# Where the split weights of the plain products begin within a 128-byte row

## The chip, the cores and the metric

The kernel runs on one core of a Trainium2 chip, as one launch. The metric is the device time of a launch in microseconds. Times of single instructions come from one profiled execution.

## The reference

One decoder layer for 512 prompt tokens and 64 new tokens (8 sequences of 8), D = 1024, all in float32. Cut to the matrix products:

```python
h = modulate(rms_norm(x, n1_g), sh1, sc1)
x = x + 0.5 * g1 * (silu(h @ w1_gate) * (h @ w1_up)) @ w1_down      # FF = 2816
h = modulate(rms_norm(x, nm_g), sh2, sc2)
u, v, q, k, rv, rg, ga, gb = split(h @ w_in)                        # 10240 columns
o_a = gelu(u) * chunk_spatial_mix(layer_norm(gelu(v)), gm_ws, gm_bs)
o_b = head_rms(retention(rotary(q), rotary(k), rv, S0)) * silu(rg)
x = x + g2 * ((sigmoid(ga) * (o_a @ w_a) + sigmoid(gb) * (o_b @ w_b)) @ w_o)
h = modulate(rms_norm(x, n2_g), sh3, sc3)
x = x + 0.5 * g3 * (silu(h @ w2_gate) * (h @ w2_up)) @ w2_down
y = rms_norm(x, final_g)
```

## The kernel before

All 576 tokens are kept side by side along the free dimension, channels on the partitions. A float32 product is made of three products in the format float32r: each operand is split into a high part (a cast, on ScalarE) and a low part (the rest, on VectorE), and high x high, high x low and low x high are summed in PSUM. Three kinds of split products make up most of the kernel.

The **plain products** are the function `proj` (its matmuls are L482 in the profile). The weights are the stationary operand, 128 x 128 of them for one matmul; the tokens are the moving operand, in two parts of 320 and 256 columns (`PART`). Here belong both down projections, `w_a`, `w_b`, `w_o` and the u columns of `w_in`. Their split weights are made by `load_w` and `split_w` (writes at L184 and L185) or by `Down` (writes at L949 and L954), which takes its tile from `home_wd`, `home_whl`, `home1`, `home_o` or `nine_w`.

The **pairs** are `prod` (L648): gate and up weights, and the columns of `w_in` for q, k and the gates, in a scheme that needs fewer block products. The weights are stationary, 288 token columns move. Their split weights are made by `Weights.put_hi` and `put_lo` (writes at L666 and L676).

The **values** are L1350, L1363 and L1580: tokens stationary, 256 weight columns moving. Their weights come from `load_w`.

Nearly all split weights lie in a tile somewhat larger than they are, and begin `INTO` = 28 elements into it, 112 bytes; `set_in` cuts that piece out. SBUF tiles are laid out so that each of these tiles starts on a multiple of 128 bytes, the pool `line` at the top of the kernel being there for that. Two smaller products of the same format are of use below: L1504 sums squares over the partitions with a tile of ones (`onesr`) as the stationary operand, and L1515 makes the new state of the 64 new tokens.

The built program has these first bytes, modulo 128:

| line | product | columns | stationary begins at | moving begins at |
|---|---|---|---|---|
| L482 | plain | 320 and 256 | 112 | 0 |
| L648 | pairs | 288 | 112 | 0 |
| L1350, L1363, L1580 | values | 256 | 0 | 112 |
| L1504 | squares | 288 | 64 | 0 |
| L1515 | new state | 256 | 0 | 0 |

The order on each engine is set by the program's text and, in three stretches, by an order written out by hand (`BEGIN`, `INTO_MIX`, `INTO_FFN2`). TensorE takes its products in that order, each with a weight load of its own ahead of it, and a product waits for the semaphores of its operands alone. Weights come in through SyncE's queue into the buffers `wraw`.

Of the kernel before, what the change touches and what calls it, by code (L numbers as in the profile page):

```python
# [9 lines left out]
F32R = mybir.dt.float32r  # L10
# [5 lines left out]
P = 128  # L16
D = 1024
KC = D // P
# [8 lines left out]
HEADS = 8  # L27
# [8 lines left out]
GROUPS = (5, 6, 5, 6)  # L36

INTO = 28
HALF = (slice(0, H), slice(H, T))
PART = (slice(0, 320), slice(320, T))  # L40
PW = (320, T - 320)
# [42 lines left out]
def layer_kernel(ctx: ExitStack, tc: tile.TileContext, a):  # L84
# [7 lines left out]
    wp = ctx.enter_context(tc.tile_pool(name="wp", bufs=1))  # L92
# [16 lines left out]
    def nm(s):  # L109
        count[0] += 1  # L110
        return f"{s}_{count[0]}"


    now = {"wraw": None, "slu": None}
    turn = [0, 0]

    def pool(stack, name, side="left"):
        return stack.enter_context(tc.tile_pool(name=nm(name), bufs=1, side=side, reuse_waits="tile"))
# [16 lines left out]

    def nine_w(shape):

        return set_in(now["xs1"], shape, 9 * 256 - shape[1] * shape[2] * shape[3], tag="x", name=nm("xw"), bufs=3)

    def half(dt=F32, w=H):  # L140
        return tp.tile([P, w], dt, tag="h", name=nm("h"), bufs=7)
# [1 line left out]
    def bank():  # L143
        return pp.tile([P, 512], F32, tag="ps", name=nm("ps"), bufs=8)

    def set_in(home, shape, room=INTO, **kw):

        n = 1
        for d in shape[1:]:
            n *= d  # L150
        t = home.tile([P, n + room], F32R, **kw)[:, INTO:INTO + n]
        if len(shape) == 4:
            return t.rearrange("p (a b c) -> p a b c", b=shape[2], c=shape[3])
        return t.rearrange("p (a b c d) -> p a b c d", b=shape[2], c=shape[3], d=shape[4])


    def raw4(shape):
        turn[0] += 1
        own = now["wraw"] is not None and turn[0] % 4 == 0
        return (now["wraw"] if own else wp).tile(  # L160
            [P] + shape, F32, tag="wraw", name=nm("wraw"), bufs=1 if own else 3
        )

    def whl(shape):
        small = len(shape) == 3 and shape[1] == 1
        tag = "whs" if small else "whl"
        return set_in(
            now["whs"] if small else wp, [P] + shape, INTO if small else 64, tag=tag, name=nm(tag), bufs=1 if small else 4
        )

    def load_raw(src, k0, kc, c0, cols):
        raw = raw4([kc, cols])
        nc.sync.dma_start(
            out=raw, in_=src[k0 * P:(k0 + kc) * P, c0:c0 + cols].rearrange("(k p) c -> p k c", p=P)
        )
        return raw

    def high_low(shape):
        t = whl([2] + shape)
        return t[:, 0], t[:, 1]  # L180

    def split_w(raw, eng=None):
        hi, lo = high_low(list(raw.shape[1:]))
        ACT.copy(out=hi, in_=raw)  # L184
        now["lo"] = (eng or DVE).tensor_tensor(out=lo, in0=raw, in1=hi.bitcast(F32), op=ALU.subtract)  # L185
        return hi, lo

    def load_w(src, k0, kc, c0, cols, eng=None):
        return split_w(load_raw(src, k0, kc, c0, cols), eng)

    def split(hi, lo, src):
        ACT.copy(out=hi, in_=src)  # L192
# [36 lines left out]
    def tick(us):  # L229
        for s in list(side):  # L230
            s[1] -= us
            while s in side and s[1] <= 0:
                try:
                    s[1] += next(s[0])
                except StopIteration:
                    side.remove(s)

    def finish(*gens):
        for s in list(side):
            if not gens or s[0] in gens:  # L240
                for _ in s[0]:
                    pass
                side.remove(s)
# [43 lines left out]
    for i in range(2):  # L287
        for n in range(NT):
            rows = P if n < 4 else NS
            t = first.tile([rows, 512], F32, name=nm("xt"))  # L290
            src = a["x_prompt"][0, n * P:(n + 1) * P] if n < 4 else a["x_sample"].rearrange("b l d -> (b l) d")
# [121 lines left out]
    class Norm:  # L413
# [4 lines left out]
        def square(self, x, h):  # L418
            if self.all is None:
                self.all = tp.tile([P, T], F32, tag="all", name=nm("all"), bufs=1)  # L420
                self.acc = [self.all[:, HALF[i]] for i in range(2)]
            first = self.n[h] == 0 and not self.t[h]
            t = self.acc[h] if first else half()
            self.t[h].append(t)
            ACT.activation(out=t, in_=x[:, HALF[h]], func=AF.Square)

# [49 lines left out]
    def proj(w, X, h, kc=KC, c0=0, ks=None, ps=None):  # L476
        ps = bank() if ps is None else ps
        wh, wl = w
        for k in ks or range(kc):
            xh, xl = X[k]  # L480
            for z, (s, m) in enumerate(((wh, xh), (wh, xl), (wl, xh))):
                PE.matmul(  # L482
                    ps[:, :PW[h]], lhsT=s[:, k, c0:c0 + P], rhs=m[:, PART[h]],
                    start=k == 0 and z == 0, stop=k == kc - 1 and z == 2,
                )
        return ps
# [5 lines left out]
    def cost(kc):  # L492
        return kc * 3 * 0.1225
# [26 lines left out]
    class Operands:  # L520
# [27 lines left out]
        def blocks(self, j):  # L548
            hb = self.hb
            return tuple(hb[:, c:c + 2, cl] for c in (2 * j, 4 + 2 * j) for cl in HALF)  # L550

# [56 lines left out]
    def norm_steps(st, n, O, h):  # L608
# [4 lines left out]
        for p in range(4):  # L613
            st[f"x{p}{h}"] = lambda p=p: O.x(p, n.r[h], HALF[h])
            for c in range(2):
                if h:
                    st[f"b{p}{c}"] = lambda p=p, c=c: O.b(2 * p + c, slice(H, NP))
                else:
                    st[f"b{p}{c}0"] = lambda p=p, c=c: O.b(2 * p + c, HALF[0])

# [76 lines left out]
    class Plain(Weights):  # L697
# [43 lines left out]
        def e0s(self):  # L741
            self.g = self.g or self.gated()
            ACT.activation(out=self.g[:, HALF[0]], in_=self.A[0][:, :H], func=AF.Silu)

# [215 lines left out]
            return self.w[c]  # L960

    def home_wd(c, shape):
        return set_in(now["hl"], shape, 64, tag="wd", name=nm("wd"), bufs=2)

    def home_whl(c, shape):
        return home_wd(c, shape) if c in (0, 1, 4, 5) else whl(shape[1:])

    def ffn(xs, wg, wu, wd, gate, p, home, last_down):

# [2 lines left out]
        for i in range(2, FC + 1):  # L972
# [8 lines left out]
            if i in ends:  # L981
                gi = ends.index(i)
                f0, n = i - GROUPS[gi], GROUPS[gi]
                W = Down(wd, f0, n, home if i == FC else home_wd)
                W[0]
                W[1]
            if i > 2:
# [7 lines left out]
            if i == FC:  # L995

                held = {}
                for c, h in LAST[:3]:
                    held[c, h] = proj(W[c], G, h, kc=n, ks=range(n - 1))

                def product(c, h):
                    if (c, h) in held:
                        return proj(W[c], G, h, kc=n, ks=[n - 1], ps=held[c, h])
                    return proj(W[c], G, h, kc=n)

# [118 lines left out]
    win = a["w_in"][0]  # L1124
    U0, V0, Q0, K0, RV0, RG0, GA0, GB0 = 0, 1024, 2048, 3072, 4096, 6144, 8192, 9216
# [5 lines left out]
    def home1(c, shape):  # L1131
        if c in (6, 7):
            return nine_w(shape)
        return home_wd(c, shape) if c in (0, 1, 4, 5) else whl(shape[1:])

    def stream_slots():

# [397 lines left out]

    def weights_b(hds, j):
        kc = 2 * len(hds)
        return load_w(a["w_b"][0], 2 * hds[0], kc, j * (8 // kc) * P, 8 // kc * P)

    def out_b(hds, j, wb, cs=None):  # L1540

# [108 lines left out]
        store()  # L1650

    def weights_u(g):
        return load_w(win, 0, KC, U0 + g * P, P)

    def gate_u(g, wu):
        t = slot([P, T])
# [118 lines left out]
            mix(g - 2)  # L1775
            tick(1.5)
    finish(prev)
    first_a = load_w(a["w_a"][0], 0, KC, 0, P)
    mix(6)
    mix(7)  # L1780
    st.close()
# [9 lines left out]
                nc.sync.dma_start(out=t[c], in_=src[:, c])  # L1791

    def last_b(j):
        wb = load_w(a["w_b"][0], 2 * HEADS - 2, 2, j * 512, 512)
        for c in range(4 * j, 4 * j + 4):
            for h in range(2):
                ps = proj(wb, OBs[HEADS - 1], h, kc=2, c0=c % 4 * P)
                t = acc[c][:, PART[h]]
                DVE.tensor_tensor(out=t, in0=ps[:, :PW[h]], in1=t, op=ALU.add)
            POOL.tensor_tensor(out=acc[c], in0=acc[c], in1=sb[c], op=ALU.mult)  # L1800
# [7 lines left out]

    def home_o(c, shape):
        if c < 2:  # L1810
            return whl(shape[1:])
        if c < 5:
            return nine_w(shape)
        return home_wd(c, shape) if c < 7 else set_in(hb_pool, shape, tag="wo", name=nm("wo"), bufs=1)

    Wo = Down(a["w_o"][0], 0, KC, home_o)
    late = []
# [1 line left out]
    def merge(c, h):  # L1819

        t = sa[c][:, PART[h]]
        DVE.tensor_tensor(out=t, in0=t, in1=acc[c][:, PART[h]], op=ALU.add)
        split(X[c][0][:, PART[h]], X[c][1][:, PART[h]], t)

    for pr in ([0], [1], [2], [3], [4], [5], [6, 7]):
        W = {c: load_w(a["w_a"][0], 0, KC, c * P, P) if c else first_a for c in pr}
        if len(pr) == 2:
            Wo[0]
            Wo[1]
        for h in range(2):  # L1830
            for c in pr:
                ps = proj(W[c], OA, h)
                t = sa[c][:, PART[h]]
                DVE.tensor_tensor(out=t, in0=ps[:, :PW[h]], in1=t, op=ALU.mult)
                if len(pr) == 2:
                    merge(c, h)
                tick(cost(KC))
        if len(pr) == 1:
            late.append(pr[0])
        if pr[0] in (1, 3):  # L1840
            last_b(pr[0] // 2)
        if pr[0] == 2:
            fetch_gates(range(4, KC))
        if pr[0] > 1:
            for c in late[:1 if pr[0] < 5 else KC]:
                late.remove(c)
                for h in range(2):
                    merge(c, h)
# [18 lines left out]
    hb_pool = pool(greg, "hb", "right")  # L1867
# [184 lines left out]
```

## Time and profile before

| | |
|---|---|
| median of 3 runs | 1671.1 us (1668.0 to 1671.6) |
| the profiled execution's own time | 1670.5 us |
| its span, first to last instruction | 1668.7 us |
| TensorE busy | 98% of the span, 12548 matmuls |
| VectorE, ScalarE, GpSimd busy | 69%, 47%, 17% |
| granted TensorE clock, mean | 0.996 |

A line of a group names the source line, the engine, the operation, the tile written and the tiles read (the moving operand first, then the stationary one), the shape and the count. A matmul's duration runs from its start to its modelled end, and matmuls overlap; the pace of a stretch is therefore read from the starts of its pieces and their counts. The timeline joins neighbours of one line and one pair of tiles into one row and prints the shape of the first; a row of L482 that says 128x320 can hold 256-column products too, where the text says so.

### The profile page before, as it was taken

The page shows a single profiled execution, that of the slowest core. Times are in us where ns is not written, and L with a number is a line of the kernel's source. Part 1 is how long each engine was busy: PE and PEld are TensorE (multiplying, and loading weights), DVE is VectorE, ACT ScalarE, POOL GpSimd, SP SyncE. Part 2 cuts the span into 40 slices and gives each one's busy share as a digit, 9 for nine tenths or more (in the row PEclk, how much of TensorE's full clock was granted, in tenths as well). Part 3 has the DMA queues.
Part 4 walks back from the last instruction along what each step waited for, and adds up shares of the span by engine and source line. Part 5 has one row for each costly group of instructions (what it writes and reads, how often), then busy time and mean ns, then how long its engine had stood idle before and what let it go on. Part 6 is the DMA issues. An engine that isn't in the chain of part 4 may idle for free. (4 is left out here: it accounts for less than half of the span.)

```text
span 1668.7 us, 31368 instructions
## 1 busy us (share of the span) xinstructions
PE 1637.5 (98%) x12548; PEld 1575.7 (94%) x12548; DVE 1154.8 (69%) x1835; ACT 784.0 (47%) x1331; POOL 291.5 (17%) x372
## 2 busy tenths in 40 slices
PE   7999999999999999999999999999999999999997
PEld 4899999999999999999999999998999999999997
DVE  6867857576696877755688554677748768576773
ACT  5634524344564556644445444443237435243454
POOL 0000000000411011113346343454131000000002
PEclk9999999999999999999999999999999999999999
DMA  9553444332537776764457474798540233332321
GB/s 303 145 153 103 140 138 129 114 102 86 177 119 210 220 219 192 222 199 166 149 176 256 156 192 148 209 257 267 163 135 17 82 92 98 92 90 85 96 86 58
DMA packets 300212, 252.09 MB, mean 151 GB/s; under 512 B 13593, under 2 KB 260633, under 8 KB 300066
## 3 DMA queue, kind: packets, MB, share of 16 engines
q1 hardware_dynamic: 284594, 206.76, 41.1%
q0 software_dynamic: 13168, 40.97, 8.8%
q10 hardware_dynamic: 2304, 2.36, 0.4%
q8 instruction: 98, 1.61, 0.4%
q14 instruction: 48, 0.39, 0.1%
HBM read 207.01 MB, written 43.02 MB: 150 GB/s over the span
## 5 line engine op out<-in xcount | busy, mean ns | idle before, releaser
L648 PE MATMUL ps<-xa,whl 128*128 128x288 f32 x3000 | 423.7, 296 | 5.5 <-ACT xa L561 2.1
L648 PEld LDWEIGHTS ps<-xa,whl 128*128 128x128 f32 x3000 | 404.7, 190 | 18.2 <-issue 4.2
L648 PE MATMUL ps<-xs,whl 128*128 128x288 f32 x2040 | 289.1, 295 | 0.8 <-ACT sn L657 0.6
L648 PEld LDWEIGHTS ps<-xs,whl 128*128 128x128 f32 x2040 | 274.0, 189 | 10.9 <-issue 4.2
L676 DVE TENSOR_TENSOR whl<-wraw,whl 128x1024 fp32r<-128x1024 f32 x192 | 234.5, 1223 | 54.2 <-ACT whl L666 48.3
L666 ACT CAST whl<-wraw 128x1024 fp32r<-128x1024 f32 x192 | 200.0, 1047 | 105.8 <-DVE wraw L790 64.6
L482 PEld LDWEIGHTS ps<-c,wd 128*128 128x128 f32 x1824 | 244.2, 189 | 3.5 <-issue 3.4
L482 PE MATMUL ps<-c,wd 128*128 128x320 f32 (+1 forms) x1824 | 247.4, 296 | 0.0
L482 PE MATMUL ps<-c,whl 128*128 128x256 f32 (+1 forms) x1368 | 191.8, 298 | 1.1 <-ACT c L192 0.7
L482 PEld LDWEIGHTS ps<-c,whl 128*128 128x128 f32 x1368 | 184.3, 189 | 3.1 <-DVE c L193 0.9
L469 POOL TENSOR_TENSOR x<-x,s 128x64 f32<-128x64 f32 x72 | 35.6, 495 | 808.6 <-DVE s L468 780.7
L463 DVE SCALAR_TENSOR_TENSOR x<-ps,gate,x 128x320 f32<-128x320 f32 (+1 forms) x128 | 61.1, 481 | 120.3 <-PE ps L482 120.3
L657 ACT COPY sn<-ps 128x288 f32<-128x288 f32 x195 | 77.4, 399 | 107.5 <-PE ps L648 107.0
L185 DVE TENSOR_TENSOR whl<-wraw,whl 128x1024 fp32r<-128x1024 f32 x56 | 77.9, 1393 | 67.4 <-ACT whl L184 67.1
L949 ACT CAST wd<-wraw 128x640 fp32r<-128x640 f32 (+2 forms) x58 | 45.3, 781 | 107.7 <-PE ps L482 98.3
L1350 PE MATMUL ps<-whl,xx 128*128 128x256 f32 x768 | 88.6, 275 | 0.0
L1350 PEld LDWEIGHTS ps<-whl,xx 128*128 128x128 f32 x768 | 87.8, 188 | 0.0
L648 PE MATMUL ps<-xs,whs 128*128 128x288 f32 x480 | 69.9, 294 | 0.0
L184 ACT CAST whl<-wraw 128x1024 fp32r<-128x1024 f32 x56 | 58.5, 1048 | 22.6 <-PE ps L482 14.5
L648 PEld LDWEIGHTS ps<-xs,whs 128*128 128x128 f32 x480 | 65.7, 189 | 0.0
L666 ACT CAST whs<-wraw 128x512 fp32r<-128x512 f32 x62 | 38.5, 621 | 55.7 <-PE ps L648 46.7
L954 DVE TENSOR_TENSOR wd<-wraw,wd 128x640 fp32r<-128x640 f32 (+2 forms) x58 | 53.4, 920 | 10.1 <-ACT wd L949 9.8
(285 smaller groups left out, 2223.1 us busy)
## 6 DMA issues: line engine op xcount, KB each, us to landing
ada<-in_w_ada_dram SPq DMA_DIRECT2D x56, 512.0 KB
wraw<-in_w_in_dram SPq DMA_DIRECT2D x96, 256.0 KB
wraw<-in_w_gate_dram SPq DMA_DIRECT2D x88, 256.0 KB
wraw<-in_w_up_dram SPq DMA_DIRECT2D x88, 256.0 KB
wraw<-in_w_in_dram SPq DMA_DIRECT2D x32, 512.0 KB
wraw<-in_w_down_dram SPq DMA_DIRECT2D x32, 384.0 KB
wraw<-in_w_down_dram SPq DMA_DIRECT2D x32, 320.0 KB
accd<-c POOLq DMA_DIRECT2D x32, 288.0 KB, 5.7
```

What stands on the lines that cost most here:

```text
L184: ACT.copy(out=hi, in_=raw)
L185: now["lo"] = (eng or DVE).tensor_tensor(out=lo, in0=raw, in1=hi.bitcast(F32), op=ALU.subtract)
L463: DVE.scalar_tensor_tensor(out=x[:, o:o + w], in0=ps[:, :w], scalar=g[:, c, 0:1], in1=x[:, o:o + w], op0=ALU.mult, op1=ALU.add)
L469: return lambda: POOL.tensor_tensor(out=x[:, NP:T], in0=x[:, NP:T], in1=u, op=ALU.add)
L482: PE.matmul(ps[:, :PW[h]], lhsT=s[:, k, c0:c0 + P], rhs=m[:, PART[h]], start=k == 0 and z == 0, stop=k == kc - 1 and z == 2,)
L648: PE.matmul(ps[:, :H], lhsT=s[:, j * P:(j + 1) * P], rhs=m[:, j, :], start=fresh and j == 0 and z == 0, stop=j == 3 and z == 2, skip_group ...
L657: ACT.copy(out=t, in_=ps[:, :H])
L666: ACT.copy(out=hl[:, 0], in_=src)
L676: now["lo"] = DVE.tensor_tensor(out=hl[:, 1], in0=src, in1=hl[:, 0].bitcast(F32), op=ALU.subtract)
L949: ACT.copy(out=hl[:, 0], in_=self.raw[c])
L954: DVE.tensor_tensor(out=lo, in0=self.raw[c], in1=hi.bitcast(F32), op=ALU.subtract)
L1350: PE.matmul(ps[:, :DV], lhsT=s, rhs=m, start=i == 0, stop=i == 23)
```

## The change

A second start, `MID` = 16 elements or 64 bytes, is added beside `INTO`. `set_in`, `whl`, `high_low`, `split_w` and `load_w` take the start as an argument, and every place that makes split weights for `proj` hands over `MID`. The pairs (`put_hi`) and the values (`load_w` of rv and v) keep `INTO`. No tile grows, since the room behind the piece stays the same in total. The built program has the same instructions in the same order on every engine; in all 4032 products of L482 the stationary operand begins 48 bytes earlier, and no other operand of a product moves.

```diff
 INTO = 28
+MID = 16
...
     def nine_w(shape):
 
-        return set_in(now["xs1"], shape, 9 * 256 - shape[1] * shape[2] * shape[3], tag="x", name=nm("xw"), bufs=3)
+        room = 9 * 256 - shape[1] * shape[2] * shape[3]
+        return set_in(now["xs1"], shape, room, MID, tag="x", name=nm("xw"), bufs=3)
...
-    def set_in(home, shape, room=INTO, **kw):
+    def set_in(home, shape, room=INTO, at=INTO, **kw):
...
-        t = home.tile([P, n + room], F32R, **kw)[:, INTO:INTO + n]
+        t = home.tile([P, n + room], F32R, **kw)[:, at:at + n]
...
-    def split_w(raw, eng=None):
-        hi, lo = high_low(list(raw.shape[1:]))
+    def split_w(raw, eng=None, at=INTO):
+        hi, lo = high_low(list(raw.shape[1:]), at)
...
     def home_wd(c, shape):
-        return set_in(now["hl"], shape, 64, tag="wd", name=nm("wd"), bufs=2)
+        return set_in(now["hl"], shape, 64, MID, tag="wd", name=nm("wd"), bufs=2)
...
-        return home_wd(c, shape) if c in (0, 1, 4, 5) else whl(shape[1:])
+        return home_wd(c, shape) if c in (0, 1, 4, 5) else whl(shape[1:], MID)
...
-        return load_w(a["w_b"][0], 2 * hds[0], kc, j * (8 // kc) * P, 8 // kc * P)
+        return load_w(a["w_b"][0], 2 * hds[0], kc, j * (8 // kc) * P, 8 // kc * P, at=MID)
...
-        return load_w(win, 0, KC, U0 + g * P, P)
+        return load_w(win, 0, KC, U0 + g * P, P, at=MID)
...
-        W = {c: load_w(a["w_a"][0], 0, KC, c * P, P) if c else first_a for c in pr}
+        W = {c: load_w(a["w_a"][0], 0, KC, c * P, P, at=MID) if c else first_a for c in pr}
```

More of the change, by code (lines that the diff above doesn't have):

```diff
@@ L162, in raw4, with whl @@
         )
-    def whl(shape):
+    def whl(shape, at=INTO):
         small = len(shape) == 3 and shape[1] == 1
@@ L167, in whl @@
         return set_in(
-            now["whs"] if small else wp, [P] + shape, INTO if small else 64, tag=tag, name=nm(tag), bufs=1 if small else 4
+            now["whs"] if small else wp, [P] + shape, INTO if small else 64, at,
+            tag=tag, name=nm(tag), bufs=1 if small else 4,
         )
@@ L176, in load_raw, with high_low @@
         return raw
-    def high_low(shape):
-        t = whl([2] + shape)
+    def high_low(shape, at=INTO):
+        t = whl([2] + shape, at)
         return t[:, 0], t[:, 1]
-    def split_w(raw, eng=None):
-        hi, lo = high_low(list(raw.shape[1:]))
+    def split_w(raw, eng=None, at=INTO):
+        hi, lo = high_low(list(raw.shape[1:]), at)
         ACT.copy(out=hi, in_=raw)
@@ L186, in split_w, with load_w @@
         return hi, lo
-    def load_w(src, k0, kc, c0, cols, eng=None):
-        return split_w(load_raw(src, k0, kc, c0, cols), eng)
+    def load_w(src, k0, kc, c0, cols, eng=None, at=INTO):
+        return split_w(load_raw(src, k0, kc, c0, cols), eng, at)
     def split(hi, lo, src):
@@ L1133, in home1 @@
             return nine_w(shape)
-        return home_wd(c, shape) if c in (0, 1, 4, 5) else whl(shape[1:])
+        return home_wd(c, shape) if c in (0, 1, 4, 5) else whl(shape[1:], MID)
     def stream_slots():
@@ L1777, in layer_kernel @@
     finish(prev)
-    first_a = load_w(a["w_a"][0], 0, KC, 0, P)
+    first_a = load_w(a["w_a"][0], 0, KC, 0, P, at=MID)
     mix(6)
@@ L1793, in last_b @@
     def last_b(j):
-        wb = load_w(a["w_b"][0], 2 * HEADS - 2, 2, j * 512, 512)
+        wb = load_w(a["w_b"][0], 2 * HEADS - 2, 2, j * 512, 512, at=MID)
         for c in range(4 * j, 4 * j + 4):
@@ L1810, in home_o @@
         if c < 2:
-            return whl(shape[1:])
+            return whl(shape[1:], MID)
         if c < 5:
             return nine_w(shape)
-        return home_wd(c, shape) if c < 7 else set_in(hb_pool, shape, tag="wo", name=nm("wo"), bufs=1)
+        return home_wd(c, shape) if c < 7 else set_in(hb_pool, shape, INTO, MID, tag="wo", name=nm("wo"), bufs=1)
     Wo = Down(a["w_o"][0], 0, KC, home_o)
```

## The prediction

> **What bounds the kernel now.** I read the page's busy table first, then what TensorE waited for, then the chain of work that ended last, and last the timeline of a few stretches without interruption, to get the time from one product to the next.
>
> ```profile
> span 1668.7 us, 31368 instructions
> PE 1637.5 (98%) x12548; PEld 1575.7 (94%) x12548; DVE 1154.8 (69%) x1835; ACT 784.0 (47%) x1331; POOL 291.5 (17%) x372
> PEclk9999999999999999999999999999999999999999
> ```
>
> TensorE is busy for 98% of the span at the full granted clock, and each of its 12548 products has a weight load of its own. No other engine comes near. Its waits for others are short; the longest sums are these:
>
> ```profile
> engine line waited for: us in total, times, longest us
> PE ps L316 <- ACT ada L310: 4.5, 3, 2.0
> PE ps L299 <- ACT ada L296: 4.3, 1, 4.3
> ```
>
> So the kernel lasts about as long as its products take one after the other, and a change that moves no instruction can act only through the time of one product. In the chain (start, us, what) the stages that the change touches stand as unbroken pieces:
>
> ```profile
> 1330.73 31.94 PE ps L482 x240
> 1429.38 38.37 PE ps L482 x288
> 1523.33 31.94 PE ps L482 x240
> ```
>
> 38.37 us for 288 products is 133.2 ns for one, and 31.94 for 240 is 133.1, so every such stage has the same pace. Half of these products are 320 columns wide and half 256. The timeline of stretches that hold one width only tells them apart (start, us, engine, line, count):
>
> ```profile
> 1634.71 5.30 PE L482 MATMUL ps<-c,wd 128*128 128x320 f32 x35
> 1639.84 5.30 PE L482 MATMUL ps<-c,whl 128*128 128x320 f32 x35
> ...
> 1203.60 5.57 PE L482 MATMUL ps<-c,whl 128*128 128x256 f32 x45
> ```
>
> From 1634.71 to 1639.84 lie 35 products of 320 columns: 5.13 / 35 = 146.6 ns. The 45 of 256 columns end 5.57 us after the first began, the last one takes 0.28 us from its start to its end, so 5.29 / 44 = 120.2 ns. Their mean, 133.4, is what the chain's pieces gave.
>
> **The change, part by part.** It adds no instruction, removes none, moves none past another, and leaves every tile where it was. What changes is the first byte of the stationary operand of the L482 products, from 112 to 64 within a row of 128 bytes; their moving operands stay at byte 0. How many these are, from the source view of L482:
>
> ```profile
> L482 PE MATMUL ps<-c,wd x1824: 277/307/495, 110.5 to 1651.5; 128*128 128x320 f32 x100, 128*128 128x256 f32 x83
> L482 PE MATMUL ps<-c,whl x1368: 276/306/500, 417.8 to 1657.7; 128*128 128x320 f32 x98, 128*128 128x256 f32 x98
> L482 PE MATMUL ps<-xx,whl x384: 276/307/500, 909.4 to 1044.7; 128*128 128x320 f32 x96, 128*128 128x256 f32 x96
> ```
>
> With the smaller groups of that view (xa,xw 144, xa,whl 96, xa,wd 96, c,xw 72, xa,wo 48) they are 4032. So one nanosecond per product is 4.03 us of the kernel, and the sum is 4032 times the change in the pace of one product, plus what ScalarE and VectorE gain or lose when they write to the new place.
>
> That second term I take as nothing. The splits are written by L184 and L185, by L949 and L954; the page has
>
> ```profile
> L184 ACT CAST whl<-wraw 128x1024 fp32r<-128x1024 f32 x56 | 58.5, 1048 | 22.6 <-PE ps L482 14.5
> L666 ACT CAST whl<-wraw 128x1024 fp32r<-128x1024 f32 x192 | 200.0, 1047 | 105.8 <-DVE wraw L790 64.6
> ```
>
> and what hides them is the products: ScalarE stands idle before these writes because it waits for TensorE or VectorE. Were each of the 56 writes of L184 to take 100 ns longer, that would be 5.6 us spread over a 47% busy engine; without that cover it would be 5.6 us on the path.
>
> The first term the trace shows only by neighbours. No L482 product has ever run with byte 64. The built program gives the first bytes within 128 of the other products that use the same number format, and the timeline gives their pace:
>
> ```profile
> 796.15 4.01 PE L1350 MATMUL ps<-whl,xx 128*128 128x256 f32 x34
> ...
> 1308.51 1.74 PE L648 MATMUL ps<-xs,whl 128*128 128x288 f32 x12
> 1311.66 1.74 PE L648 MATMUL ps<-xs,whl 128*128 128x288 f32 x12
> ...
> 890.58 0.69 PE L1504 MATMUL ps<-c,onesr 128*128 128x288 f32 x4
> 891.10 1.12 PE L1515 MATMUL ps<-c,c 128*128 128x256 f32 x8
> 892.06 1.75 PE L482 MATMUL ps<-c,whl 128*128 128x256 f32 x13
> ...
> 941.71 0.69 PE L1504 MATMUL ps<-c,onesr 128*128 128x288 f32 x4
> 942.24 1.12 PE L1515 MATMUL ps<-c,c 128*128 128x256 f32 x8
> ```
>
> The values (L1350: stationary at 0, moving at 112, 256 columns) take (4.01 - 0.275) / 33 = 113.2 ns; the 0.275 us is the page's mean of one. L1515 (stationary at 0, moving at 0, 256 columns) takes (892.06 - 891.10) / 8 = 120.0 ns. L482 with its stationary at 112 and its moving at 0 took 120.2. The pairs (L648: 112 and 0, 288 columns) take (1311.66 - 1308.51) / 24 = 131.2 ns. And L1504, the only product with its stationary at 64 and its moving at 0, 288 columns, takes 0.52 / 4 = 130 ns in one place and 0.53 / 4 = 132.5 in the other.
>
> Two comparisons change the stationary start alone. From 0 to 112 at 256 columns: 120.0 against 120.2. From 112 to 64 at 288 columns: 131.2 against 130 to 132.5. In both it moves next to nothing. The one comparison that moves much, L1350 against L1515, 6.8 ns, has another moving start. Hence the value I take: zero per product, with both ends kept. The lower end is the pace of L1350: 113.2 - 120.2 = -7.0 ns, times 4032, -28.2 us. The upper end is the slower reading of L1504, 132.5 - 131.2 = +1.3 ns, or +5.2 us; this row is the nearest, since it has exactly the two starts that the change makes.
>
> The Trainium skill, "TensorE: Matmul & The Clock Gate", section "Step-by-step: what each phase is for", says that TensorE has two independent read ports into SBUF, so that loading the next weights takes nothing from the running matmul; by that rule no start of the stationary operand could matter and the sum would be exactly zero. The trace does not bear the rule out as a whole: two products of 256 columns, both at full clock, differ by 6.8 ns with the layout alone. What it leaves open is whether the stationary start has a part in that.
>
> The sum: 1670.5 us (the profiled execution's own time, 1.8 us above its span) + 4032 x 0 = 1670.5. The runs had a median of 1671.1 and a lowest of 1668.0, so I say **1670**.
>
> **The rivals.** *The relation of the two starts counts, not the moving start alone (faster).* Moving minus stationary, modulo 128, is 112 for L1350 (113.2 ns), 16 for L482 now (120.2), 0 for L1515 (120.0), and becomes 64 for L482. If the load's reading and the product's reading get in each other's way only when they stand close together in the row, 64 is as far apart as can be. Halfway between the two paces is -3.5 ns: 4032 x -3.5 = -14.1 us, 1656; the whole way is 1642. For it: the quick L1350 is the one with a large distance. Against it: L1504 has the distance 64 and is no quicker than L648 with 16. TensorE would turn nearly all of it into time within a stage, since L482's stages have no wait inside. Some would be given back just behind a stage, where the chain leaves TensorE:
>
> ```profile
> 1505.18 3.19 DMA wraw<-in_w_down_dram
> 1512.04 11.29 PE ps L648 x84
> ```
>
> There a weight transfer is late next; its length, 3.2 us, at the three such places in the chain bounds what could be given back at about 10 us of the larger gain.
>
> *The load at 64 falls in step with the product's reading and holds it longer (slower).* The place is L482's stages, the price the upper reading of L1504: +1.3 ns, 1670.5 + 5.2 = 1675.7; at twice that, 1681. It decides from 0.8 ns per product on (3.3 us / 4032). For it: the slower of the two readings above. Against it: the other reading of the same row, 130, is below L648's 131.2, and a reading of four products is good to 2.5 ns only.
>
> *The change does not do what it says.* It would need a tile whose start isn't a multiple of 128 bytes. In the built program all 4032 stationary operands move by 48 bytes and nothing else does, so this gets no chance of its own.
>
> **How the numbers follow.** A measurement of this kernel tells no change from one within about 0.2%, 3.3 us, which is 0.8 ns per product. No change: 0.41, because both comparisons of the stationary start point there. Faster: 0.38, because 6.8 ns of layout cost are shown to be there to be had, and one row of four products is thin evidence that byte 64 has no part in it; most of this chance lies between 1655 and 1667, a quarter of it or so below. Slower: 0.21, mostly up to 1678. The likeliest case alone spans 1667 to 1674. The range that holds the time 8 times in 10 leaves out the far end of the faster case and the double price of the slower one: 1650 to 1678.
>
> **What would show it right or wrong.** In the changed kernel's timeline the stretch of 35 products from 1634.71 would again take 5.13 us and the down stage of 288 again 38.4 us: then the stationary start has no part, and L1350's pace comes from the moving start. If 320 columns fall towards 140 ns and 256 towards 113, the distance of the two starts is what counts. If they rise past 148 and 121.5, the slower rival holds. L648's 131.2 and L1350's 113.2 should stay in every case; if they move too, the cause is elsewhere. The prediction is wrong if the pace of L482 changes by more than 0.8 ns, and its reasoning is wrong if the time moves while that pace does not.

## The result and the profile after

The changed kernel takes 1662.9 us (median of 8 runs, 1661.2 to 1667.3) against 1670.9 for the kernel before (8 runs): a ratio of 0.9959, 95% interval 0.9947 to 0.9972. It is faster by 0.41%. The forecast was no change, at 1670, with 1667 to 1674 as the likeliest band; the time lies outside that band, inside the stated range and in the band of the faster rival.

The line numbers of the changed kernel are three higher: L485 are the plain products, L651 the pairs, L1353, L1366 and L1583 the values. Its page begins:

```profile
span 1660.9 us, 31368 instructions
PE 1628.6 (98%) x12548; PEld 1566.4 (94%) x12548; DVE 1153.0 (69%) x1835; ACT 783.1 (47%) x1331; POOL 293.4 (18%) x372
```

The span is 7.8 us shorter, and TensorE's busy time has shrunk by 8.9. The waits have not changed in kind. In a line of the chain stand the start in us, the length in us and what it was. The down stages in the chain:

```profile
1325.37 31.21 PE ps L485 x240
1423.21 38.08 PE ps L485 x288
1516.88 31.22 PE ps L485 x240
```

240 products take 31.21 us in place of 31.94: 130.0 ns for one, not 133.1. The stage of 288 takes 38.08 in place of 38.37: it gained 0.29 us where its neighbours gained 0.73, although it has the same kind of products at the same starts. This difference comes back below. The timeline of stretches of one width (start, us, engine, line, count):

```profile
1627.14 5.44 PE L485 MATMUL ps<-c,wd 128*128 128x320 f32 x36
1632.41 5.29 PE L485 MATMUL ps<-c,whl 128*128 128x320 f32 x35
...
1200.32 5.35 PE L485 MATMUL ps<-c,whl 128*128 128x256 f32 x44
...
1249.78 4.24 PE L485 MATMUL ps<-xa,wd 128*128 128x256 f32 x36
1253.86 2.88 PE L485 MATMUL ps<-xa,wo 128*128 128x256 f32 x24
1256.58 3.36 PE L651 MATMUL ps<-xs,whl 128*128 128x288 f32 x24
...
1358.01 1.74 PE L651 MATMUL ps<-xa,whl 128*128 128x288 f32 x12
1359.58 1.74 PE L651 MATMUL ps<-xs,whl 128*128 128x288 f32 x12
```

320 columns: (1632.41 - 1627.14) / 36 = 146.4 ns, where it was 146.6. 256 columns: (5.35 - 0.28) / 43 = 117.9 ns in the stretch at 1200, but (1253.86 - 1249.78) / 36 = 113.3 in the one at 1250, and (1256.58 - 1253.86) / 24 = 113.3 again for the w_o products behind it. Before, the stretch of this width that the prediction shows took 120.2. The pairs stand where they stood, 1.57 / 12 = 131 ns.

Taken over all products from the starts in the two traces, from one product's start to the next one's: the 2016 products of 256 columns took 246.2 us and take 239.0 (-7.2), the 2016 of 320 columns 303.8 and 303.2 (-0.6), the pairs 777.1 and 776.1 (-1.1); the rest took 1 us more. So the gain is the plain products of 256 columns and hardly anything else. Their mean pace, leaving out intervals over 165 ns, which hold a wait, fell from 119.4 to 115.5 ns. It has two parts: in the changed kernel 51% of these intervals are 112 to 115 ns and 47% are 116 to 119, with 2% above; before, 15% and 44%, with 41% above. A run of products settles near one of two paces, 113.4 or 117.8: of the 106 unbroken runs of 12 or more such products, 62 have a mean below 114.7 and the other 44 one of 117.3 to 118.4.

### The profile page after: what moved, and what is told of

Its sections match the earlier page's. It is cut to its first block, busy times and chain, and to the rows that moved or that the text cites. A ratio compares the mean times of both kernels' runs of the same rounds, so it can differ in the third digit from the quotient of the medians.

```text
span 1660.9 us, 31368 instructions
## 1 busy us (share of the span) xinstructions
PE 1628.6 (98%) x12548; PEld 1566.4 (94%) x12548; DVE 1153.0 (69%) x1835; ACT 783.1 (47%) x1331; POOL 293.4 (18%) x372
## 5 line engine op out<-in xcount | busy, mean ns | idle before, releaser
L651 PE MATMUL ps<-xa,whl 128*128 128x288 f32 x3000 | 422.2, 295 | 6.0 <-ACT xa L564 2.6
L651 PEld LDWEIGHTS ps<-xa,whl 128*128 128x128 f32 x3000 | 403.1, 190 | 18.7 <-issue 5.0
L651 PE MATMUL ps<-xs,whl 128*128 128x288 f32 x2040 | 289.1, 295 | 0.8 <-ACT sn L660 0.6
L651 PEld LDWEIGHTS ps<-xs,whl 128*128 128x128 f32 x2040 | 274.0, 189 | 11.0 <-issue 5.0
L485 PEld LDWEIGHTS ps<-c,wd 128*128 128x128 f32 x1824 | 240.1, 188 | 3.5 <-issue 3.4
L485 PE MATMUL ps<-c,wd 128*128 128x320 f32 (+1 forms) x1824 | 243.3, 294 | 0.0
L485 PE MATMUL ps<-c,whl 128*128 128x256 f32 (+1 forms) x1368 | 189.6, 296 | 1.1 <-ACT c L195 0.7
L485 PEld LDWEIGHTS ps<-c,whl 128*128 128x128 f32 x1368 | 182.0, 188 | 3.3 <-ACT c L195 1.0
L1353 PE MATMUL ps<-whl,xx 128*128 128x256 f32 x768 | 88.9, 276 | 0.0
L1353 PEld LDWEIGHTS ps<-whl,xx 128*128 128x128 f32 x768 | 88.1, 188 | 0.0
L651 PE MATMUL ps<-xs,whs 128*128 128x288 f32 x480 | 69.9, 294 | 0.0
L651 PEld LDWEIGHTS ps<-xs,whs 128*128 128x128 f32 x480 | 65.7, 189 | 0.0
```

Source lines behind the costliest of these rows:

```text
L485: PE.matmul(ps[:, :PW[h]], lhsT=s[:, k, c0:c0 + P], rhs=m[:, PART[h]], start=k == 0 and z == 0, stop=k == kc - 1 and z == 2,)
L651: PE.matmul(ps[:, :H], lhsT=s[:, j * P:(j + 1) * P], rhs=m[:, j, :], start=fresh and j == 0 and z == 0, stop=j == 3 and z == 2, skip_group ...
L1353: PE.matmul(ps[:, :DV], lhsT=s, rhs=m, start=i == 0, stop=i == 23)
```

## The experiments

Theories at the outset. *Distance*: what counts is moving start minus stationary start within 128 bytes, as in the prediction's faster rival. *Byte*: 112 was a bad start for a stationary operand, and others are good. *Width*: the effect belongs to products of 256 columns. All kernels are built on the changed one. Ratios are to the kernel before, in runs on the same chip, and two kernels of different sessions are compared by these ratios; "pace" is the mean from start to start as above.

**Stationary start at 0.**

```diff
-MID = 16
+MID = 0
```

> The stationary operand of the 4032 plain products begins at byte 0 of a row in place of 64. Distance theory (what counts is moving start minus stationary start within 128 bytes; here 0, as in L1515): the 256-column products go back to about 120 ns, the 320-column ones stay at 146 to 147, the kernel goes back to about 1670. Byte theory (112 was a bad place for a stationary operand and any other is a good one): 256 columns stay near 115.5 ns, the kernel near 1663.

Ratio 1.0010 (1.0001 to 1.0019), median 1671.8 us. Pace 119.7 ns for 256 columns, 146.7 for 320. In its timeline

```profile
1206.52 5.68 PE L485 MATMUL ps<-c,whl 128*128 128x256 f32 x46
```

is (5.68 - 0.28) / 45 = 120.0 ns, and 1700 of the 1992 intervals of this width in wd, whl and xw tiles are exactly 120 ns. The byte theory falls: 0 is no better than 112. The distance theory stands. The run also shows that the gain hangs on this start: with it moved and nothing else, the kernel is back at the time of before.

**The same byte 64, one row further on.**

```diff
-MID = 16
+MID = 48
...
-set_in(hb_pool, shape, INTO, MID, tag="wo", ...)
+set_in(hb_pool, shape, INTO, 16, tag="wo", ...)
```

> Stationary operands begin 192 bytes into their tiles in place of 64: again byte 64 of a 128-byte row, but of the neighbouring row, so that the place within 256 bytes is 64 and not 192, while the moving operand keeps its place. Distance within 128 bytes: nothing changes, 115.5 ns for 256 columns, 1663. Distance within 256 bytes: all plain products of 256 columns take the 113.3 ns that the 24 w_o products with that place take in the changed kernel, 2.2 ns x 1992 = -4.4 us, 1658.5; 320 columns unchanged at 146.6.

Ratio 0.9986 (0.9976 to 0.9995), median 1666.7. Pace 117.6 ns for 256 columns, 146.6 for 320. Neither expectation: the quick pace is not everywhere, it is almost gone. 118, 117 and 119 ns make up 1877 of the 2016 intervals, 113 and 114 only 91. So the place within more than 128 bytes matters. In the built program the moving operand of all these products lies at 128 within 256 bytes; their stationary operand lies at 192 in the changed kernel and at 64 here. And the w_o products, whose 24 products of 256 columns have the same tile and the same start as in the changed kernel:

```profile
1256.37 2.99 PE L485 MATMUL ps<-xa,wo 128*128 128x256 f32 x24
1259.19 3.06 PE L651 MATMUL ps<-xs,whl 128*128 128x288 f32 x22
```

(1259.19 - 1256.37) / 24 = 117.5 ns, where the changed kernel had 113.3. Only what ran ahead of them is laid out differently. The same products at the same addresses have two paces, and which one they take went with the layout of what ran ahead.

**The pairs at 64 as well.**

```diff
-            hl = whl([2, len(names), 512])
+            hl = whl([2, len(names), 512], MID)
```

> On top of the change the stationary operands of the 5784 pair products (288 columns) begin at byte 64 too. Distance theory with the same effect at any width: 131.2 falls by 2 to 4 ns, -12 to -23 us, 1640 to 1651. Width theory (the gain at 256 columns is particular to that width, as 320 columns gained next to nothing): 288 columns move by at most 1 ns in either direction, as the four products of L1504 did, 1657 to 1669.

Ratio 0.9981 (0.9972 to 0.9990), median 1667.0. The pairs' pace is 132.2 ns against 131.3 in the changed kernel, 0.85 ns more; times 5784 this is 4.9 us; by the ratios the kernel lost 0.22%, 3.7 us. Byte 64 does harm to the pairs, and by about what L1504 showed in the kernel before, where its unbroken groups of four take 132.0 to 132.2 when the starts are not rounded to 10 ns. The width theory's forecast, at most 1 ns either way, holds. But width isn't the only difference: the pairs' moving operands lie by turns at 0 and at 128 within 256 bytes, those of the plain products always at 128. The plain products were not touched, yet their stage of 288 products is quicker than in the changed kernel:

```profile
1330.74 31.90 PE L485 MATMUL ps<-c,wd 128*128 128x320 f32 x240
1429.36 37.66 PE L485 MATMUL ps<-c,wd 128*128 128x320 f32 x288
1522.59 31.90 PE L485 MATMUL ps<-c,wd 128*128 128x320 f32 x240
```

against the changed kernel's

```profile
1325.20 31.38 PE L485 MATMUL ps<-c,wd 128*128 128x320 f32 x240
1423.05 38.24 PE L485 MATMUL ps<-c,wd 128*128 128x320 f32 x288
1516.72 31.38 PE L485 MATMUL ps<-c,wd 128*128 128x320 f32 x240
```

37.66 for 38.24, and 31.90 for 31.38: the stage of 288 has gone from the slower pace to the quicker one, the two of 240 the other way. The pairs run directly ahead of these stages, and nothing else was changed in the layout. It is the same finding as at w_o, in stages of 240 and 288.

**The values' moving weights at 64.**

```diff
-return [load_w(win, 4 * kk, 4, V0 + i * 512 + z * 256, 256) for kk in range(2)]
+return [load_w(win, 4 * kk, 4, V0 + i * 512 + z * 256, 256, at=MID) for kk in range(2)]
...
-wv = [load_w(win, 4 * i, 4, RV0 + hd * DV, DV) for i in range(2)]
+wv = [load_w(win, 4 * i, 4, RV0 + hd * DV, DV, at=MID) for i in range(2)]
```

> On top of the change the moving weights of the value products (L1350, L1363, L1580 of the kernel before; 1344 products of 256 columns, stationary at 0) begin at byte 64 in place of 112. Distance theory (64 is as far apart as can be, in whichever direction): 113 to 115.5 ns, the kernel within 3 us of the changed one. Theory that the moving start must lie at the end of a row: 120 ns, +6.6 x 1344 = +8.9 us, 1672.

Ratio 0.9989 (0.9980 to 0.9999), median 1667.9. In the timeline

```profile
899.76 4.40 PE L1353 MATMUL ps<-whl,xx 128*128 128x256 f32 x36
```

is (4.40 - 0.275) / 35 = 117.9 ns; the mean over the 1344 value products is 117.8, against 114.1 in the changed kernel, where

```profile
794.92 10.25 PE L1353 MATMUL ps<-whl,xx 128*128 128x256 f32 x89
```

is (10.25 - 0.275) / 88 = 113.4. +3.7 x 1344 = 5.0 us, and 0.30% by the ratios is 5.0 us too. So for these products the moving start has a part: it alone was changed. With the distance 64 the values stand at the slower of the two paces that the plain products have with it. Both theories miss, the distance theory by 2.3 ns and the other by 2.2.

This kernel also settles whether the choice between the two paces is mere chance of one execution. Its plain products are laid out as in the changed kernel and run in the same order. Before the first value product and after 1160 us lie 79 of their runs of 256 columns, and 78 of them have the pace of the changed kernel to 0.5 ns. Its down stages repeat those of the changed kernel:

```profile
1330.30 31.38 PE L485 MATMUL ps<-c,wd 128*128 128x320 f32 x240
1428.05 38.24 PE L485 MATMUL ps<-c,wd 128*128 128x320 f32 x288
1521.65 31.38 PE L485 MATMUL ps<-c,wd 128*128 128x320 f32 x240
```

Of the 53 runs between, in the stretch where the value products run, 38 kept their pace and 15 did not. So the pace is repeated from one execution to another, and nearly all that changed it lies where the kernel was changed.

**Stationary start at 16, 32, 96.** Each is the line `MID = 16` with 4, 8 or 24.

> Plain products' stationary operands begin at byte 16 (moving minus stationary 112, as in the value products L1350). Distance theory: 256 columns take 113.4 to 114 ns as L1350 does, 1.7 ns below the changed kernel's 115.6, -3.4 us, about 1659.5; 320 columns 146.6. Theory that L1350's pace comes from its moving start: byte 16 is near byte 0, 119 to 120 ns, 1671.

> Plain products' stationary operands begin at byte 32 (moving minus stationary 96). Distance theory: between the paces at 64 and at 112, so 113.5 to 115.6 ns for 256 columns, 1659 to 1663. Theory that byte 64 of a row is a special place: 119 to 120 ns, 1671.

> Plain products' stationary operands begin at byte 96 (moving minus stationary 32). Distance theory: between the paces at 64 (115.6) and at 16 (119.4), so 116 to 119 ns for 256 columns, 1664 to 1670. Theory that byte 64 of a row is a special place: 119 to 120 ns, 1671.

| start | moving minus stationary, within 128 | 256 columns, ns | 320 columns, ns | ratio to before |
|---|---|---|---|---|
| 16 | 112 | 118.4 | 146.7 | 0.9984 (0.9973 to 0.9995) |
| 32 | 96 | 118.3 | 146.8 | 0.9990 (0.9979 to 1.0001) |
| 96 | 32 | 118.6 | 146.8 | 0.9989 (0.9979 to 1.0000) |

At byte 16 the distance within 128 bytes is that of the values, which take 113.8 in the kernel before; the plain products take 118.4:

```profile
1202.27 5.49 PE L485 MATMUL ps<-c,whl 128*128 128x256 f32 x45
```

(5.49 - 0.28) / 44 = 118.4. The distance theory falls here, and at 32 too, as long as the distance is taken within 128 bytes. In its place comes the *point theory*: the other starts are alike to within 1.5 ns (118.3 to 119.7), and 64 alone has the quick pace often.

A distance within 256 bytes is not refuted by this. In the built program it is 112 for the values (stationary at 128, moving at 240), but 240 for the plain products at byte 16. Where two kinds of products share such a distance, they agree to within 0.7 ns: at 0 the new state (L1515) takes 119.0 in the kernel before and the plain products 119.7 in the kernel with start 0; at 64 the plain products of the next-row kernel take 117.6 and the values of the kernel above 117.8. Against it stand the 24 w_o products, also at distance 64, with 113.3 in the changed kernel. No run gave the plain products the distance 112 throughout, which a start of 144 bytes into the tile would do (in the last experiment a part of them has it, by turns with 240); this rival stays untested.

**The pairs at 16.** In `put_hi`, `whl([2, len(names), 512], 4)`.

> On top of the change (plain products at 64) the pairs' stationary operands begin at byte 16 in place of 112 (moving minus stationary 112 in place of 16). Distance theory at any width: 288 columns fall from 131.2 by 2 ns or more, -12 us, 1651 or less. Width theory: within 1 ns of 131.2 as at byte 64 (132.2 there), 1657 to 1669.

Ratio 1.0003 (0.9992 to 1.0013), median 1671.7. The pairs take 133.4 ns, 2.0 more than at 112 and outside both expectations: +2.0 x 5784 = 11.6 us, and the kernel lost 0.44% by the ratios, 7.4 us, against the changed one. Part of the difference is the plain products, whose 256 columns came to 115.0 here. For the pairs the order is 112 (131.3), 64 (132.2), 16 (133.4). As with the pairs at 64, the untouched plain stage of 288 ran at the quick pace (37.66 us).

**Around 64: 48, 80, 72.** `MID` = 12, 20, 18.

> Plain products' stationary operands begin at byte 48, 16 bytes before the place of the change. In the changed kernel each run of 256-column products settles at one of two paces, 113.4 or 117.8 ns. Point theory (the quick pace exists at byte 64 alone): 118 to 120 ns, 1667 to 1671. Window theory (the quick pace exists in the middle of the row): 113.4 to 116 ns, 1659 to 1663.

> The same at byte 80, 16 bytes behind the place of the change. Point theory: 118 to 120 ns, 1667 to 1671. Window theory: 113.4 to 116 ns, 1659 to 1663.

> The same at byte 72, 8 bytes behind the place of the change. Point theory: 118 to 120 ns, 1667 to 1671. Window theory: 113.4 to 116 ns, 1659 to 1663; with byte 80 slow and byte 72 quick the window is less than 16 bytes on this side.

| start | 256 columns, ns | 320 columns, ns | ratio to before |
|---|---|---|---|
| 48 | 119.0 | 145.7 | 0.9996 (0.9985 to 1.0007) |
| 72 | 118.5 | 146.7 | 0.9998 (0.9989 to 1.0008) |
| 80 | 118.7 | 146.3 | 0.9987 (0.9977 to 0.9997) |

The point theory holds on the three, within the one row in which they were tried: a start 8 bytes beyond 64 already loses the quick pace. The profiled execution of the kernel with 48 was 4 us quicker than its median and the one with 72 1 us, so nothing is made of the order of the three among themselves.

**The values' layout for pairs and for a down projection.** Stationary at 0 and moving at 112 for all pairs and for the 1056 products of the second down projection. To make room, the tiles of the split weights lose 128 bytes and those of the moving operands gain 128.

```diff
-            t = nine("xs1" if name in ops["near"] else "xa", [P, 2, 4, H])
+            t = nine("xs1" if name in ops["near"] else "xa", [P, 8 * H + 32])[:, INTO:INTO + 8 * H]
...
-            hl = whl([2, len(names), 512])
+            hl = whl([2, len(names), 512], 0)
...
-now["whs"] if small else wp, [P] + shape, INTO if small else 64, at,
+now["whs"] if small else wp, [P] + shape, 0 if small else 32, at,
...
-return set_in(now["hl"], shape, 64, MID, tag="wd", name=nm("wd"), bufs=2)
+return set_in(now["hl"], shape, 32, now.get("down_at", MID), tag="wd", name=nm("wd"), bufs=2)
...
-            self.G = slot([P, T], F32R), slot([P, T], F32R)
+            room, at = (32, INTO) if "down_at" in now else (0, 0)
+            self.G = tuple(slot([P, T + room], F32R)[:, at:at + T] for _ in range(2))
```

> On top of the change the value products' layout, stationary at byte 0 and moving at byte 112, is given to all 5784 pair products (288 columns) and to the 1056 plain products of the second down projection (320 and 256 columns). Moving-start theory (the quick pace of L1350 belongs to its moving operand's start, and holds at any width): the second down projection takes 113.4 ns for 256 columns and about 140 for 320, the pairs about 126.7 in place of 131.2; -26 us from the pairs, -4.6 us from the down projection, about 1632 to 1640. Theory that it holds at 256 columns alone: 113.4 there, 146.6 and 131 to 133 elsewhere, 1660 to 1672.

Ratio 1.0020 (1.0011 to 1.0030), median 1672.9. The pairs take 132.1 ns, the down projection 117.8 for 256 columns and 146.9 for 320, so neither expectation came true. But the values, whose bytes within a row this kernel leaves at 0 and 112, have lost their quick pace as well:

```profile
900.40 3.80 PE L1355 MATMUL ps<-whl,xx 128*128 128x256 f32 x31
```

(3.80 - 0.28) / 30 = 117.3 ns, 117.7 over all 1344. What changed in their own layout is that tiles now come at odd multiples of 128 bytes, so that from one product to the next the place within 256 bytes differs, where it was always the same. The same holds for the plain products outside the second down projection, still at 64 and 0 within a row: 18% of their intervals at 256 columns are 112 to 115 ns, where 46% were in the changed kernel. So the experiment doesn't tell whether the moving start is what made L1350 quick; it shows that a quick pace can also be lost without any change of these products within the 128-byte row. The pairs ahead of them were laid out differently too, and what share that has isn't shown.

## Why the prediction was right or wrong

**What bounds the kernel: right.** Products one after the other; the span fell by 7.8 us, and the plain products' intervals account for that. No wait took the gain back, not even at the three places that the prediction named: the late weight transfers in the chain are 3.4, 3.2 and 3.4 us long, and were 3.5, 3.2 and 3.3.

**4.03 us per nanosecond: right as a conversion.** A mean of -3.9 ns at 256 columns and -0.2 to -0.4 at 320 over 2016 products each is 8.3 to 8.7 us; the sums of all intervals, those with waits among them, fell by 7.8.

**The value taken, zero per product: wrong.** This is the step that failed. The time lies inside the range only because the range was drawn wide enough for the faster rival. The value rested on two comparisons of the stationary start alone, 0 against 112 at 256 columns and 112 against 64 at 288. Both readings were good only to the rounding of the starts: unrounded, the row of L1515 that the prediction shows takes 119.4 in place of 120.0, and L1504 takes 132.0 to 132.2 in place of 130 to 132.5. Both comparisons were borne out to within 1 ns: the start at 0 gave 1671.8 us, and byte 64 gave the pairs 132.2 ns for 131.3. What failed was to carry them over to byte 64 at 256 columns. Neither row held that combination, and in the one row in which the starts were tried, the effect is at this byte and this width and nowhere else; at byte 64 of the next row it is mostly gone (117.6 ns). "The nearest row" had the right two starts within 128 bytes and the wrong width, and its moving operand lies by turns at two places within 256 bytes, which the prediction did not look at.

**The faster rival: right in sign, twice too large, and its reason fails as stated.** It had -14 us at half the way; measured are -7 to -8. Half of it is missing because the rival let 320 columns gain as much as 256, and they gained a tenth. Its distance rule, within 128 bytes, falls with byte 16 (118.4 ns at the distance at which the values take 113.8). That the time lies in its band is luck as far as that rule goes.

**The slower rival** had the pairs' case: byte 64 does hold the pairs, at 288 columns, longer, by 0.85 ns. It was put at the wrong products.

**The rule of two independent read ports**, which the prediction takes from the Trainium skill ("TensorE: Matmul & The Clock Gate", section "Step-by-step: what each phase is for"), would, as the prediction applied it, have made every start alike. For 320 columns the traces agree with that to within 1.3 ns over all starts (145.7 to 147.0); at 256 columns the stationary start alone is worth up to 4 ns in the mean (115.5 against 119.7), so the measurement decides against "no start could matter". It doesn't show that the two reads get in each other's way: the recorded length of a weight load in the largest groups of the plain products has a median of 188 ns before and after.

**What would show it right or wrong** served in part. By its own bound of 0.8 ns the prediction is wrong: 7.8 us over 4032 products is 1.9 ns. 320 columns did not fall towards 140, part of 256 did fall to 113, and the pairs and values stayed. But the two signs that it named for no change nearly came true all the same: 35 products of 320 columns take 35 x 146.4 = 5.12 us for 5.13, and the down stage of 288 takes 38.08 for 38.4. One stands for a width that gained a tenth as much, the other settled at the slower pace. Two stretches were too few for a cost that takes two values.

**What stays open.** Why a run settles at 113.4 or at 117.8 at byte 64, why 320 columns have no such choice, and whether the moving start, which has a part at the values, acts alone or by its distance from the stationary one within 256 bytes. The runs show that what ran ahead and the place within 256 bytes bear on the pace; the mechanism in the memory or in TensorE was not shown. No tried kernel beat the changed one.

## What to carry to other kernels

Where TensorE is the bound and each product has its own weight load, the byte at which an operand starts was here worth some nanoseconds per product, and it has to be tried for each kind of product by itself, with the place within 256 bytes and not only within 128: the best start for the plain products (64) was a worse one than 112 for the pairs. A neighbouring row of the profile with the same starts and another width was no evidence here. Compare such kernels by the histogram of the time from start to start, not by the mean alone, since a product can have two paces, and look at several stretches.

## What had not been expected of the hardware

The same 24 products at the same addresses took 113.3 ns each in one kernel and 117.5 in another that differed only in what ran ahead of them, and a stage of 288 products took 38.24 or 37.66 us in the same way; a third kernel, with the same products ahead as the first, repeated the 38.24. A start 8 bytes off the good one (72 for 64) cost 3 ns of 115.5. And the value products lost 3.6 ns (114.1 to 117.7) in a kernel that moved tiles by 128 bytes and gave other products another layout, with every start of theirs within its 128-byte row unchanged.
